# Inversion blocks and inverses read by GpSimd's queue, a chain with fewer slots, and state reads behind the inverses' read

## The chip, the cores and the metric

The kernel runs on one core of a Trainium2 chip. The metric is the device time of one execution in microseconds (us). Names used throughout: PE is TensorE, DVE is VectorE, ACT is ScalarE, POOL is GpSimd, SP is SyncE, which only issues transfers here. SPq, ACTq and POOLq are the queues in which SP, ACT and POOL issue DMAs. POOL is also a compute engine, and it takes its DMAs and its arithmetic from one queue, in order.

## The reference

One inference step of a recurrent decoder trunk with two layers, width 2048, for a prompt of 256 tokens and 8 sample sequences of 8 tokens each, 320 rows in all. What matters here is the first layer, with a gated delta rule of 8 heads (128 x 128) and a gated linear attention (GLA) of 4 heads (128 x 256):

```
proj = rmsnorm(x) @ w_in                  # 2048 -> 7,200 columns
# gated delta rule, per head and per chunk of C tokens
A   = strictly_lower((k * beta) @ k.T * decay)
sol = solve_triangular(A + I, rhs)        # unit diagonal, C x C
v_new = u - w @ S ;  o = (q * exp(G)) @ S + (q @ k.T * decay) @ v_new
S   = S * exp(g_last) + k_dec.T @ v_new
# GLA, per head and per chunk
o = (q * exp(B)) @ S + tril(...) @ v ;  S = diag(exp(b_last)) * S + k_dec.T @ v
x = x + concat(o_a, o_b) * silu(gates) @ w_out
```

The second layer is a gated linear recurrence (RG-LRU) between two more dense products. Every input and result is float32; the outputs are both groups' tokens and all new states.

## The kernel before

**The dense products.** All dense weights (2048 x 512 columns a group, 30 groups of 8 chunks) are streamed from DRAM by SP in chunks of 512 KB (`wst`, line 214). ACT copies each half to float32r (`wh`, line 248), DVE makes the rest (`wl`, line 249), and PE runs three products of 128 x 128 by 128 x 320 for each block: `xh` with `wh`, `xl` with `wh`, `xh` with `wl` (line 381). That is 192 products a group and 5,760 in the loop of line 381. The last group is made by lines 268 to 355.

**The work around them.** All other work is written as Python generators in four lists. After every third dense product `slot()` advances the first generator of each list by one step. Between its steps a generator waits as many slots as the table WAITS has for that place (`yield from wait("invert32.1")`), so that one entry of the table is a delay of three dense products. A scheduler then orders each engine's instructions by that order, by priorities and by what it holds the durations to be; PE executes what it finds in its queue, in order, and stands still if an operand is late. `add_manual_dep(... NoSync ...)` gives the scheduler an order and puts no semaphore into the program.

**The delta rule's inverses.** The prompt's 8 heads are done in two halves of 4 heads, each with two chunks of 128 tokens, c = 0 and 1 (`delta_half`, `quad_prompt`). For a half:

- `quad_a` turns k, q and v, forms k k^T (`kk`, line 786) and k q^T (`kq`, line 798), and writes the four 32 x 32 diagonal blocks of each of its 4 matrices to DRAM (`bd_scratch`, line 793, SP).
- `invert32` reads them back in another layout (`ab`, line 823, four reads), inverts the 32 x 32 blocks by 31 pairs of POOL operations (lines 831 and 833), and writes the inverses to DRAM (`xd_scratch`, line 838, four writes on POOL).
- `load_inv` reads them twice: into `XT` as diagonal blocks (line 871) and into `xc` (line 876).
- `quad_front` builds the 128 x 128 inverse from them: DVE turns `xc` (lines 909 and 919), PE makes `lp` (line 915), DVE copies it to `xp` (line 907), PE makes `lxt` from `xp` and `XT` (lines 925 and 927), and a second, larger step follows (lines 935 and 940). `quad_b` uses the result (`y`, `po`, `sn`, `ks`).

The samples' 8 heads (`delta_sample`) have blocks of 8 x 8, which DVE inverts (line 857 to 861); their inverses go through `xt_scratch` (line 865) into `XT` (line 874). `pq` multiplies the states (`st`, 2 x 512 KB a pair of heads, two buffers, line 1027), and `y` (line 1072) needs `XT` and what DVE makes of `pq`. This is done for two pairs of heads one behind the other.

**GLA's samples.** For each of two pairs of heads: states `st` from DRAM (line 1464), `gpo` (lines 1489 and 1491), then in `gla_out` ACT's square (line 1287), two POOL operations (1288, 1289), DVE's `gon` (1292) and PE's transposes `got` (1296).

**The sum of squares.** Behind the fourth output group, DVE ends the sum `sqa` (line 1594), from which PE makes `r1ps` (line 449) in `row_rstd`.

Of the kernel before, what the change touches and what calls it, by code (L numbers as in the profile page):

```python
# [7 lines left out]
F32 = mybir.dt.float32  # L8
# [6 lines left out]
P = 128  # L15
# [51 lines left out]
def wait(name):  # L67
    for _ in range(WAITS[name]):
        yield
# [3 lines left out]
def hybrid_step(ctx, tc, x_cols, x_rows, w_head, w_dense, w_small, w_lr, w_gate, par_a, par_b, par_c, gains, last_gain,  # L73
# [52 lines left out]
    def behind(i):  # L126
        tc.add_manual_dep(i.ins, marks[-1].name, mybir.DependencyInfo(
            mybir.DependencyClass.NoSync, mybir.DependencyReason.DATA), reason="issue_after")

# [23 lines left out]
    ident = const.tile([P, P], F32, name="ident")  # L153
# [311 lines left out]
    def row_rstd(sq, out, nm):  # L465

        ps = bank4(nm + "ps")
        token_sums(ps, sq, True, True)
        yield from wait("row_rstd.1")
        yield from row_from(ps[:, 0:3, 0], out, nm)  # L470
# [342 lines left out]
    def invert32(ws, first):  # L813
# [8 lines left out]
        for r in range(4):  # L822
            sp.dma_start(ab[32 * r:32 * r + 32].rearrange("p i c -> p (i c)"), bass.AP(
                tensor=bd_d.tensor, offset=bd_d.offset + first * 4 * n * n, ap=[[n * n, 4 * U], [1, n * n]]))
# [42 lines left out]
    def load_inv(q, ws):  # L867
        if q.n == 32:
            for b in range(4):
                bs = slice(32 * b, 32 * b + 32)  # L870
                sp.dma_start(q.xt[bs, :, bs], xd_d[q.id:q.id + 4, b].rearrange("u c i -> c u i"))
        else:
            q.xt = ws.tile([P, 4, P], F32, name="XT", tag="XT")
            sp.dma_start(q.xt, xt_d.rearrange("u p c -> p u c"))
            return
        sp.dma_start(q.xc, xd_d[q.id:q.id + 4].rearrange("u b c i -> (b c) u i"))

# [67 lines left out]
    def quad_b(q, ws, half, c):  # L945
# [13 lines left out]
        ps = bank4("y0")  # L959
        for u in range(U):  # L960
            pe.matmul(ps[:, u, :], q.xt[:, u, :], q.rv[:, u, :], start=True, stop=True)  # L961
# [27 lines left out]
    def delta_half(half):  # L989
        with tc.tile_pool(name=f"gdn{half}", bufs=1, side="right", reuse_waits="tile") as ws:  # L990
# [8 lines left out]
            for c, q in enumerate(qs):  # L999
                q.xt, q.xc = [t_[:, 4 * c:4 * c + 4] for t_ in (xt, xc)]  # L1000
                load_inv(q, ws)
            z = ws.tile([P, 8, 96], F32, name="xz", tag="ab", bufs=1)
            pool.memset(z, 0.0)
            pt = [ws.tile([P, 4, 64], F32, name="xp", tag=tag) for tag in ("xi", "xt")]
            for p_ in pt:
                pool.memset(p_, 0.0)
            yield from wait("quad_b.1")
            yield from quad_front(qs, z[:, :, :64], z[:, :, 64:], pt, xt, xc)
# [5 lines left out]
    def delta_sample():  # L1014
# [3 lines left out]
        with tc.tile_pool(name="gdns", bufs=1, side="right", reuse_waits="tile") as ws:  # L1018
# [4 lines left out]
            def load(u):  # L1023
                st = ws.tile([P, 2, 8, P], F32, name="st", tag="ST", bufs=2)
                sts[u] = st
                for e in range(2):
                    behind(sp.dma_start(st[:, e], state_delta[2 * u + e]))
            load(0)
# [17 lines left out]
            for pr in range(2):  # L1046
# [7 lines left out]
                for v in range(2):  # L1054
                    for a in range(2):
                        for w in range(2):
                            for p in range(4):
                                pe.matmul(pq[32 * p:32 * p + 32, 2 * v + a, :], ms[v][:, a, p, 32 * w:32 * w + 32],
                                          sts[u0 + v][:, a, 2 * p + w, :], start=(v == a == w == 0), stop=False,
                                          tile_position=(0, 32 * p), skip_group_check=True)  # L1060
                for v in range(2):
# [39 lines left out]
                ps = bank4("ot")  # L1101
                for v in range(2):
                    pe.transpose(ps[:, v, :], on[:, v, :], ident)
                for e in range(2):
# [348 lines left out]
    def gla():  # L1453
# [4 lines left out]
        with tc.tile_pool(name="glas", bufs=1, side="right", reuse_waits="tile") as ws:  # L1458
            t = lambda nm, shape, bufs=1: ws.tile(shape, F32, name=nm, tag=nm, bufs=bufs)
            for su in range(2):  # L1460
# [22 lines left out]
                dve.tensor_mul(m, cm, flat(qs16)[:, None, :].to_broadcast([P, 4, P]))  # L1483
                yield from wait("gla.4")
                po = bank("gpo")
# [80 lines left out]
    def evac_res(m):  # L1566
# [16 lines left out]
        def sumsq():  # L1583
# [12 lines left out]
            env["done"].add(("x", m))  # L1596
            if m == 3:
                yield from row_rstd(env["sqa"], rb1, "r1")
                env["done"].add("r1")
                yield from wait("evac_res_sumsq.4")  # L1600
# [499 lines left out]
```

## Time and profile before

| | |
|---|---|
| median of 3 runs | 971.31 us (969.76 to 971.74) |
| profiled execution, device time | 970.0 us |
| its span, first to last instruction | 968.2 us |
| PE busy | 955.2 us, 99% of the span |
| POOL busy | 126.9 us, 13% |
| HBM read, written | 160.02 MB, 14.67 MB |
| granted TensorE clock | 0.998 |

How to read it: the span is what the trace covers, and the device time of the same execution is 1.8 us longer. A row of a group or of the timeline has line, engine, operation, output <- inputs, partitions x elements, count, and what the engine's idle time before it ended with. A row of the chain of waits has the start, the length and what it is. A row of the waits has who waited for whom, then the sum, the number and the longest in us. A row of the windows has the stretch, its length, the busy time of PE, of its weight loads (PEld), DVE, ACT and POOL (with the number of instructions that start in it), the granted clock, the share of the DMA engines and GB/s. Matmuls are pipelined, so a small gap between two of them need not show as idle.

### The profile page before, as it was taken

The numbers are of one execution on the slowest core, as the hardware profiler recorded it, in microseconds if no ns is written. First come the engines' busy times: TensorE is split into PE (matmuls) and PEld (weight loads), VectorE is DVE, ScalarE is ACT, GpSimd is POOL, SyncE is SP. The second block draws the span as 40 slices with busy tenths as digits, with TensorE's granted clock in tenths as the row PEclk, the third lists the DMA queues.
The fourth block names the chain that finished last, engine by engine and source line by source line (L and its number), as shares of the span: only waits on it lengthen the run. The fifth ranks groups of instructions, "written<-read, shape, count | busy, mean of one in ns | idle before, by whom it ended". The sixth has DMA issues, their size and how long they took to land.

```text
span 968.2 us, 18733 instructions
## 1 busy us (share of the span) xinstructions
PE 955.2 (99%) x6942; PEld 939.6 (97%) x6942; DVE 684.0 (71%) x1507; ACT 539.4 (56%) x1094; POOL 126.9 (13%) x294
## 2 busy tenths in 40 slices
PE   9999999999999999999999999999999999999997
PEld 8999999999999998999989999999999999999996
DVE  7599887666545565788667778667969668865763
ACT  6767864547233444876434346348685885434452
POOL 3010108303380011120100000100010000000000
PEclk9999999999999999999999999999999999999999
DMA  9854454523554376444588776645435335578742
GB/s 319 303 174 138 136 150 141 167 92 124 156 159 141 108 231 213 119 138 131 180 307 291 233 246 208 219 155 151 155 119 194 131 114 183 190 273 264 249 156 108
DMA packets 67618, 175.89 MB, mean 182 GB/s; under 512 B 16248, under 2 KB 25208, under 8 KB 67016
## 3 DMA queue, kind: packets, MB, share of 16 engines
q1 hardware_dynamic: 62904, 164.61, 52.7%
q0 software_dynamic: 2560, 8.65, 2.3%
q10 hardware_dynamic: 2064, 1.45, 0.5%
q8 instruction: 54, 0.88, 0.4%
q14 instruction: 36, 0.29, 0.1%
HBM read 160.02 MB, written 14.67 MB: 180 GB/s over the span
## 4 chain that ended last, share of the span: by engine, by line
PE 97%; DMA 2%; DVE 1%; ACT 0%; issue 0%; SPq 0%; POOL 0%; DVEq 0%; ACTq 0%; POOLq 0%
PE acc L381 83%; PE acc L268 3%; DMA wst<-in_w_dense_dram 1%; DMA XT<-xt_scratch 1%; PE fbt L311 1%; PE lg L1678 0%; PE lg L1677 0%; PE lg L1676 0%; PE kq L798 0%; PE kk L786 0%; PE usn L1188 0%; PE po L970 0%; PE y L961 0%; PE gpo L1489 0%; DMA wst<-in_w_head_dram 0%; PE sn L975 0%
## 5 line engine op out<-in xcount | busy, mean ns | idle before, releaser
L381 PE MATMUL acc<-xh,wh 128*128 128x320 f32 x1856 | 580.6, 313 | 0.9 <-ACT wh L235 0.9
L381 PE MATMUL acc<-xl,wh 128*128 128x320 f32 x1856 | 573.9, 310 | 0.0
L381 PE MATMUL acc<-xh,wl 128*128 128x320 f32 x1856 | 572.8, 309 | 0.0
L248 ACT ACTIVATE wh<-wst 128x512 fp32r<-128x512 f32 x479 | 279.2, 624 | 294.8 <-PE acc L381 234.3
L249 DVE TENSOR_TENSOR wl<-wst,wh 128x512 fp32r<-128x512 f32 x479 | 316.9, 691 | 166.2 <-ACT wh L248 165.3
L381 PEld LDWEIGHTS acc<-xh,wh 128*128 128x128 f32 x1856 | 348.6, 188 | 3.7 <-ACT wh L235 1.3
L381 PEld LDWEIGHTS acc<-xl,wh 128*128 128x128 f32 x1856 | 348.5, 188 | 0.7
L381 PEld LDWEIGHTS acc<-xh,wl 128*128 128x128 f32 x1856 | 348.1, 188 | 0.1
L587 DVE SCALAR_TENSOR_TENSOR yc<-slab,pa,yc 128x344 f32<-128x344 f32 x72 | 40.8, 578 | 1.8 <-ACT yc L101 1.5
L831 POOL TENSOR_TENSOR tmp<-ab,xi 128x60 f32<-128x60 f32 (+24 forms) x62 | 23.5, 378 | 55.7 <-DMA wst<-in_w_dense_dram 27.5
L833 POOL TENSOR_TENSOR xi<-xi,tmp 128x60 f32<-128x60 f32 (+24 forms) x62 | 25.5, 412 | 4.9
L1252 POOL DMA_DIRECT2D out_s_gla_dram<-ugt x8 | 4.4, 544 | 113.5 <-DVE ugt L1249 113.5
L1218 POOL DMA_DIRECT2D out_s_delta_dram<-ust x8 | 5.9, 744 | 99.6 <-DVE ust L1215 99.6
L268 PE MATMUL acc<-xl,wh 128*128 128x320 f32 (+1 forms) x64 | 18.7, 292 | 0.0
L268 PE MATMUL acc<-xh,wl 128*128 128x320 f32 (+1 forms) x64 | 18.6, 291 | 0.0
L591 ACT ACTIVATE qkv<-yc 128x256 f32<-128x256 f32 x24 | 9.9, 414 | 15.6 <-DVE yc L587 15.6
L268 PE MATMUL acc<-xh,wh 128*128 128x320 f32 (+1 forms) x64 | 18.6, 291 | 0.0
L1215 DVE SCALAR_TENSOR_TENSOR ust<-ust,es,usn 128x128 f32<-128x128 f32 x64 | 18.1, 340 | 0.1
L1636 DVE SCALAR_TENSOR_TENSOR yc<-slab,pb,yc 128x344 f32<-128x344 f32 x32 | 17.5, 570 | 0.7 <-ACT yc L1634 0.5
L478 DVE TENSOR_TENSOR slab<-acc,rb 128x256 f32<-128x256 f32 x36 | 15.0, 416 | 3.5 <-PE acc L381 3.3
L101 ACT ACTIVATE yc<-slab,pa 128x344 f32<-128x344 f32 x24 | 13.7, 578 | 4.7 <-DVE slab L479 4.5
L1705 POOL MEMSET aa<- 128x32 f32 x4 | 0.7, 171 | 117.7 <-ACT rr L1692 66.7
(464 smaller groups left out, 989.3 us busy)
## 6 DMA issues: line engine op xcount, KB each, us to landing
wst<-in_w_dense_dram SPq DMA_DIRECT2D x237, 512.0 KB, 3.8
st<-in_state_delta_dram SPq DMA_DIRECT2D x8, 512.0 KB, 5.8
st<-in_state_gla_dram SPq DMA_DIRECT2D x4, 1024.0 KB, 4.8
ust<-in_state_delta_dram SPq DMA_DIRECT2D x8, 512.0 KB, 7.5
out_s_delta_dram<-ust POOLq DMA_DIRECT2D x8, 512.0 KB, 6.0
ugt<-in_state_gla_dram SPq DMA_DIRECT2D x8, 512.0 KB
out_s_gla_dram<-ugt POOLq DMA_DIRECT2D x8, 512.0 KB, 4.0
xtok<-in_x_rows_dram SPq DMA_DIRECT2D x6, 512.0 KB, 6.1
```

The lines of the kernel that those rows point to most:

```text
L101: return act.activation(out, in_, AF.Identity, scale=scale)
L248: act.activation(h, wst[i][:, a, :], AF.Copy)
L249: env["last_split"] = dve.tensor_sub(l, wst[i][:, a, :], h.bitcast(F32))
L268: mm = pe.matmul(accs[f][:, cols], w[:, fs], x[:, cols], start=(k == 0 and j == 0), stop=(k == KT - 1 and j == 2), skip_group_check=True)
L381: mm = pe.matmul(o, (h, h, l)[j][:, fs], (xh, xl, xh)[j][k], start=(k == 0 and j == 0), stop=(k == KT - 1 and j == 2))
L478: dve.tensor_mul(xp[:, 3:259], xp[:, 3:259] if acc is None else acc[:, :256], rb[:, :256])
L587: dve.scalar_tensor_tensor(y[:, :n], xp[:, j:j + n], pa[:, ft, j:j + 1], y[:, :n], op0=OP.mult, op1=OP.add)
L591: act.activation(st["t"][:, f, :], y[:, :TP], AF.Silu)
L831: behind(pool.tensor_mul(tv, ab[:, j, j + 1:, None].to_broadcast([P, m, w]), xi[:, j:j + 1, :w].to_broadcast([P, m, w])))
L833: behind(pool.tensor_add(xi[:, j + 1:, :w], xi[:, j + 1:, :w], tv))
L1215: dve.scalar_tensor_tensor(s_, s_, es[:, col:col + 1], ps[b][:, r, :], op0=OP.mult, op1=OP.add)
L1636: dve.scalar_tensor_tensor(y[:, :n], xp[:, j:j + n], pb[:, ft, 2 + j:3 + j], y[:, :n], op0=OP.mult, op1=OP.add)
```

## The change

- **Queues.** The four `ab` reads of a half go from SP's queue to POOL's. The inverses are read on POOL's queue too, and for both chunks of a half at once: one read of `xc` (1,024 runs of 128 bytes) and four of `XT` (256 runs each) in place of two and eight. They are issued behind the memsets of `xz` and `xp`.
- **Slots.** invert32.1 from 18 to 3, invert32.2 from 15 to 13, quad_a.7 from 9 to 6, quad_b.1 from 23 to 20; gla.4 from 16 to 20, with a delay of its own for GLA's second pair (gla.5, 11); evac_res_sumsq.3 is new, 2 slots ahead of `row_rstd`.
- **State reads.** The samples' first four `st` reads have no place in the order given any more; the later four are ordered behind the `XT` read.
- **Order on PE.** The matmuls `y` of a quad in reverse order, `pq` of the second pair behind the first pair's transposes, and those transposes in reverse order.

```
@@ WAITS (changed entries only) @@
-    "quad_a.7": 9, "invert32.1": 18, "invert32.2": 15, "quad_b.1": 23, "gla.4": 16
+    "quad_a.7": 6, "invert32.1": 3, "invert32.2": 13, "quad_b.1": 20, "gla.4": 20, "gla.5": 11,
+    "evac_res_sumsq.3": 2
...
+    def order(i, j):
+        tc.add_manual_dep(i.ins, j.ins.name, mybir.DependencyInfo(
+            mybir.DependencyClass.NoSync, mybir.DependencyReason.DATA), reason="issue_after")
...
         yield from wait("invert32.1")
         for r in range(4):
-            sp.dma_start(ab[32 * r:32 * r + 32].rearrange("p i c -> p (i c)"), bass.AP(
+            pool.dma_start(ab[32 * r:32 * r + 32].rearrange("p i c -> p (i c)"), bass.AP(
                 tensor=bd_d.tensor, offset=bd_d.offset + first * 4 * n * n, ap=[[n * n, 4 * U], [1, n * n]]))
...
     def load_inv(q, ws):
-        if q.n == 32:
-            for b in range(4):
-                bs = slice(32 * b, 32 * b + 32)
-                sp.dma_start(q.xt[bs, :, bs], xd_d[q.id:q.id + 4, b].rearrange("u c i -> c u i"))
-        else:
-            q.xt = ws.tile([P, 4, P], F32, name="XT", tag="XT")
-            sp.dma_start(q.xt, xt_d.rearrange("u p c -> p u c"))
-            return
-        sp.dma_start(q.xc, xd_d[q.id:q.id + 4].rearrange("u b c i -> (b c) u i"))
+        q.xt = ws.tile([P, 4, P], F32, name="XT", tag="XT")
+        q.read = sp.dma_start(q.xt, xt_d.rearrange("u p c -> p u c"))
+
+    def load_blocks(first, xt, xc):
+        us = slice(first, first + 8)
+        pool.dma_start(xc, xd_d[us].rearrange("u b c i -> (b c) u i"))
+        for b in range(4):
+            bs = slice(32 * b, 32 * b + 32)
+            pool.dma_start(xt[bs, :, bs], xd_d[us, b].rearrange("u c i -> c u i"))
...
-        for u in range(U):
+        for u in reversed(range(U)):
             pe.matmul(ps[:, u, :], q.xt[:, u, :], q.rv[:, u, :], start=True, stop=True)
...
             for c, q in enumerate(qs):
-                q.xt, q.xc = [t_[:, 4 * c:4 * c + 4] for t_ in (xt, xc)]
-                load_inv(q, ws)
+                q.xt = xt[:, 4 * c:4 * c + 4]
...
             for p_ in pt:
                 pool.memset(p_, 0.0)
+            load_blocks(8 * half, xt, xc)
             yield from wait("quad_b.1")
...
                 for e in range(2):
-                    behind(sp.dma_start(st[:, e], state_delta[2 * u + e]))
+                    i = sp.dma_start(st[:, e], state_delta[2 * u + e])
+                    if u > 1:
+                        order(i, q.read)
+                        behind(i)
...
-                                pe.matmul(pq[32 * p:32 * p + 32, 2 * v + a, :], ms[v][:, a, p, 32 * w:32 * w + 32],
-                                          sts[u0 + v][:, a, 2 * p + w, :], start=(v == a == w == 0), stop=False,
-                                          tile_position=(0, 32 * p), skip_group_check=True)
+                                i = pe.matmul(pq[32 * p:32 * p + 32, 2 * v + a, :], ms[v][:, a, p, 32 * w:32 * w + 32],
+                                              sts[u0 + v][:, a, 2 * p + w, :], start=(v == a == w == 0), stop=False,
+                                              tile_position=(0, 32 * p), skip_group_check=True)
+                                if pr:
+                                    order(i, q.turned)
...
-                for v in range(2):
-                    pe.transpose(ps[:, v, :], on[:, v, :], ident)
+                for v in (1, 0):
+                    q.turned = pe.transpose(ps[:, v, :], on[:, v, :], ident)
...
-                yield from wait("gla.4")
+                yield from wait("gla.5" if su else "gla.4")
...
             if m == 3:
+                yield from wait("evac_res_sumsq.3")
                 yield from row_rstd(env["sqa"], rb1, "r1")
```

How the instructions move. SP's queue around the reads of the first half's inverses, before the change:

```order
L214 DMA wst<-in_w_dense_dram 128x1024 x6
L871 DMA XT<-xd_scratch 32x4x32 x4
L876 DMA xc<-xd_scratch 128x4x32
L871 DMA XT<-xd_scratch 32x4x32 x4
L876 DMA xc<-xd_scratch 128x4x32
L214 DMA wst<-in_w_dense_dram 128x1024 x2
```

POOL's queue at the same place in the change (`xp` and `xz` are the front's operands, `slab` belongs to a dense group):

```order
L1006 MEMSET xz 128x768
L839 COPY xt<-xi 128x256
L842 DMA xd_scratch<-xt 256x1x32 x4
L1009 MEMSET xp 128x256 x2
L877 DMA xc<-xd_scratch 128x8x32
L880 DMA XT<-xd_scratch 32x8x32 x4
L509 MEMSET slab 128x4x3
L510 COPY slab<-pa 128x4x8x3
```

The ten reads leave SP's queue, and five stand on POOL's, behind the writes that they read from and ahead of the slab's memset. SP's queue around the samples' inverses, before:

```order
L850 DMA ab<-bt_scratch 16x8x8 x4
L214 DMA wst<-in_w_dense_dram 128x1024 x2
L865 DMA xt_scratch<-ab 16x8x8 x4
L214 DMA wst<-in_w_dense_dram 128x1024
L1027 DMA st<-in_state_delta_dram 128x1024
L874 DMA XT<-xt_scratch 128x4x128
L1027 DMA st<-in_state_delta_dram 128x1024 x3
```

and in the change:

```order
L854 DMA ab<-bt_scratch 16x8x8 x4
L218 DMA wst<-in_w_dense_dram 128x1024
L1125 DMA kt_scratch<-ktm 4x32x128 x2
L218 DMA wst<-in_w_dense_dram 128x1024 x2
L869 DMA xt_scratch<-ab 16x8x8 x4
L873 DMA XT<-xt_scratch 128x4x128
L1031 DMA st<-in_state_delta_dram 128x1024 x4
```

The read of `XT` now follows the `xt_scratch` writes at once, and all four state reads come behind it. On PE the same matmuls are issued, at other places between the dense products. The number of dense products of line 381 (385 in the change) that PE has ahead of the first matmul named:

| matmul | before | in the change |
|---|---|---|
| half 0: second `kq`, `lp`, `lxt` | 734, 1171, 1191 | 734, 1092, 1099 |
| half 1: second `kq`, `lp`, `lxt` | 1391, 1827, 1837 | 1316, 1674, 1681 |
| samples, first pair: `pq`, `y` | 2109, 2133 | 1947, 1993 |
| samples, second pair: `pq`, `y` | 2184, 2208 | 2022, 2046 |
| GLA's samples, first pair: `gpo`, `got` | 2752, 2762 | 2615, 2637 |
| GLA's samples, second pair: `gpo`, `got` | 2799, 2809 | 2670, 2688 |
| `r1ps` | 3552 | 3558 |

8 rows, old and new, of the table WAITS are left out of this document.

## The prediction

> **What bounds the kernel now.** I read the page's busy row and its chain first, then PE's waits, then PE's idle time window by window.
>
> ```profile
> PE 955.2 (99%) x6942; PEld 939.6 (97%) x6942; DVE 684.0 (71%) x1507; ACT 539.4 (56%) x1094; POOL 126.9 (13%) x294
> PE 97%; DMA 2%; DVE 1%; ACT 0%; issue 0%; SPq 0%; POOL 0%; DVEq 0%; ACTq 0%; POOLq 0%
> ```
>
> The chain is TensorE from end to end. No matmul is added or removed, so only the 13.0 us in which PE is idle (968.2 - 955.2) can be won, and any new wait on PE costs its full length. The next two views say who ends that idle time and where it lies.
>
> ```profile
> PE y L1072 <- DMA XT<-xt_scratch: 2.4, 1, 2.4
> PE frs L353 <- DVE rr L351: 1.4, 1, 1.4
> PE got L1296 <- DVE gon L1292: 1.2, 2, 0.6
> PE warm L1831 <- DVE mhalf L1815: 1.1, 1, 1.1
> PE acc L381 <- ACT wh L235: 0.9, 1, 0.9
> PE r1ps L449 <- DVE sqa L1594: 0.5, 1, 0.5
> ```
>
> ```profile
> 0.00:10.00 10.00, 8.04 (x44) 7.64 (x45) 5.69 (x13) 6.03 (x11) 5.26 (x14) 1.00 0.80 234
> 360.00:380.00 20.00, 17.62 (x170) 16.89 (x169) 12.26 (x36) 9.43 (x22) 2.65 (x7) 1.00 0.69 226
> 490.00:510.00 20.00, 18.77 (x157) 16.81 (x156) 15.49 (x39) 6.28 (x13) 1.28 (x3) 1.00 0.95 353
> 610.00:620.00 10.00, 9.50 (x67) 9.23 (x66) 5.26 (x8) 3.15 (x6) 0.89 (x1) 1.00 0.84 306
> 950.00:968.20 18.20, 11.26 (x74) 9.62 (x72) 9.13 (x20) 5.27 (x13) 0.73 (x1) 0.90 0.38 144
> ```
>
> The start (1.96 us idle) and the end (6.94) are not touched. Three middle windows hold 20 - 17.62 = 2.38, 20 - 18.77 = 1.23 and 10 - 9.50 = 0.50 us: the waits for XT, got and r1ps. That is 4.11 us, and the change reaches all three.
>
> **The sample inverses, XT (2.38).** The chain of waits around 363 us, the timeline's rows ahead of it, and two rows of DMA landings:
>
> ```profile
> 361.35 0.20 DVE L861 COPY ab<-xi 64x64 f32<-64x64 f32 x1
> 361.58 1.75 SPq L865 DMA_DIRECT2D xt_scratch<-ab  x4
> 363.33 1.05 PE pq L1058 x32
> 364.40 0.35 SPq L1027
> 364.93 6.25 DMA XT<-xt_scratch
> 371.31 0.68 PE y L1072 x4
> 380.56 1.89 PE pq L1058 x64
> xt_scratch<-ab SPq DMA_DIRECT2D x4, 4.0 KB, 1.5
> DMA to landing us min/median/max: 4.4/4.8/7.1
> ```
>
> On SP a 512 KB state read stands ahead of the XT read and is held until pq has freed its buffer (364.38), so XT goes out at 364.93 and its 256 KB share the DMA engines with that read. In the change the XT read stands right behind the xt_scratch writes and all four state reads behind it. The last write is issued near 362.9 and lands 1.5 us later, so XT can go out near 364.5 instead of 364.93; with the same 6.25 us it lands 9.4 us behind the copy's start at 361.35. In PE's order y now stands 46 dense products behind pq instead of 24. A product costs 0.1467 us (64.09 / 437, quoted below), so even if pq again starts 1.98 us behind that copy, y falls due at 1.98 + 1.05 + 46 x 0.1467 = 9.8 us, and later if pq does. The wait ends without any help from a faster read: -2.38. What is late next are the state reads, which the second pq needs. The last goes out about 6 us behind the copy and lands at most 7.1 later, at 13; the second pq stands 75 products behind the first (11.0 us) with 2.6 us of other matmuls between, at 15.6. Covered by 2.6 us.
>
> **The GLA output, got (1.23), and r1ps (0.50).**
>
> ```profile
> 488.46 0.63 PE gpo L1491 x2
> 491.17 0.44 PE got L1296 x2
> 125.36 64.09 PE acc L381 x437
> ```
>
> From the end of gpo (489.09) to got are 2.08 us: ScalarE's square, two GpSimd operations, VectorE's gon. PE has ten products there, 1.47 us, so it waits 0.61; the second pair is alike. In the change 22 and 18 products stand between, 3.23 and 2.64 us, both over 2.08: -1.23. r1ps moves six products back, 0.88 us against a wait of 0.50: -0.50. Neither moves a DMA.
>
> **The block inversions' reads on POOL (cost 0 to 6.6, taken as 0).** This is where the change can lose. Per half it takes four ab reads and ten reads of the inverses off SP and puts four and five on POOL, and it shortens the way from the second kq to lp from 437 products (half 0) and 436 (half 1) to 358, 52.5 us. Timeline rows of POOL and SP in both halves, PE's chain rows, and the landings of POOL's xd_scratch writes:
>
> ```profile
> 130.21 0.31 SPq L823 DMA_DIRECT2D ab<-bd_scratch  x1
> 144.93 0.39 POOL L831 TENSOR_TENSOR tmp<-ab,xi 128x31 f32<-128x31 f32 x1 [27.50 <-DMA wst<-in_w_dense_dram]
> 176.90 2.60 POOL L838 DMA_DIRECT2D xd_scratch<-xt  x4 [0.31 <-POOL xt L835]
> 182.36 0.31 POOL L1006 MEMSET xp<- 128x256 f32 x1 [2.54 <-DMA xd_scratch<-xt]
> 242.01 63.94 PE acc L381 x436
> 256.52 0.61 POOL L831 TENSOR_TENSOR tmp<-ab,xi 128x31 f32<-128x31 f32 x1 [23.55 <-DMA ab<-bd_scratch]
> 286.87 2.42 POOL L838 DMA_DIRECT2D xd_scratch<-xt  x4 [0.30 <-POOL xt L835]
> 290.69 0.31 POOL L1006 MEMSET xp<- 128x256 f32 x1 [1.08 <-DMA xd_scratch<-xt]
> L838 POOL DMA_DIRECT2D xd_scratch<-xt x8: 596/630/847, 176.9 to 288.6; - x8
> DMA to landing us min/median/max: 1.9/3.0/4.1
> ```
>
> Half 0: the blocks are in DRAM at 130.21, when SP's first read got through. Four issues on POOL at 0.65 and a landing of 2.4 behind the last issue's end (3.0 - 0.6) start the inversion at 135.2 instead of 144.93. From its first operation to the first xd_scratch write are 176.90 - 144.93 = 31.97 us: 167.2. To the landing another 5.46: 172.6, and 0.3 for the memset: 172.9. The xc read moves 1024 runs where an xd_scratch write moves 256. No row has that; bounds are 0.65 (runs are free) and 2.6 (four times), and I take 1.4, nearer to the one-write row. xc lands at 176.7, and two transposes (0.89, below) make lp ready at 177.7. It is due at 125.36 + 52.5 = 177.9. The four XT reads add 2.6: landed at 179.3, against lxt's due time of 177.9 + 0.6 + 7 x 0.1467 = 179.5. Both fit by 0.2 us.
>
> Half 1: the blocks again 4.85 us behind kq's end (130.21 - 125.36; the change leaves no weight load between those writes), inversion start at 9.8, then 286.87 - 256.52 = 30.35 and 3.82 + 0.3: 44.3; XT landed at 50.7 against 54.1. Slack 3.4.
>
> The bounds: with the fastest landing (1.9) everything is early, worth nothing since PE waits for none of it now. With 0.85 per issue, 3.4 for xc and 4.1 for landings, ab is 1.6 late and the last XT read 3.5 more: 5.1 - 0.2 = 4.9 stall in half 0, 5.1 - 3.4 = 1.7 in half 1, 6.6 together. I take 0, the median rows. The relief of SP earns nothing: PE waits for no weight load. Queued behind the waiting reads on POOL are the slab's memset and copy, which come earlier than now, as the whole chain does.
>
> **A tighter front (+0.8).** The front's lp and lxt stand closer.
>
> ```profile
> 303.32 0.89 DVE L909 STREAM_TRANSPOSE xz<-xc 32x256 f32<-32x256 f32 x2
> 305.95 0.63 PE lp L915 x32
> 306.58 1.66 PE acc L381 x10
> 306.95 1.00 DVE L907 COPY xp<-lp 32x128 f32<-32x128 f32 x4
> ```
>
> From lp's end to lxt are 1.66 us, filled by ten products (1.47 unhindered, so 0.19 is lost already). Seven give 1.03: 0.63 short, or 0.26 if the copies start 0.37 sooner. Two halves less the 0.19: 0.3 to 1.1, taken as 0.8, since VectorE has weight differences ahead of the copies again.
>
> **Sum.** -2.38 - 1.23 - 0.50 + 0.8 = -3.3. The span goes from 968.2 to 964.9, the profiled execution from 970.0 to 966.7. The median of the runs shown is 1.3 above that execution, so the forecast is 968.0.
>
> **Rivals.**
>
> *The inverses come late.* For it: the 0.2 us of slack in half 0, on a landing whose row spreads from 1.9 to 4.1. Against it: half 1's slack, and reads that no longer share a queue with weight loads. Half of the bound, 2.5 us, gives 970.5: within 0.2% of the median, which is about what a measurement of this kernel can tell from no change.
>
> *The change doesn't do what it says at XT.* If XT still waits, because the read itself stays at 6.25 us or longer and pq starts early, or the state reads stop the second pq instead, 2 us come back: 970.0. Against it stand the 22 added products (3.2 us).
>
> *Slower: POOL issues are held up by VectorE.*
>
> ```profile
> L831 POOL TENSOR_TENSOR tmp<-ab,xi x62: 205/298/825, 144.9 to 284.4; 128x60 f32<-128x60 f32 x6, 128x28 f32<-128x28 f32 x4, 128x54 f32<-128x54 f32 x4, 128x48 f32<-128x48 f32 x4
> ```
>
> One and the same operation takes 205 to 825 ns, so POOL is held up at times. If its reads take twice the 0.65 us (and xc 2.8), each half is 2.6 + 1.4 + 2.6 = 6.6 us later: 6.4 stall in half 0, 3.2 in half 1, 977.6. It decides once a half is about 4.5 us late, a read at 1.1 us: then 4.3 + 1.1 eat the gain of 3.3 and 0.2% more. Against it: the eight xd_scratch writes, issued while VectorE split weights, never took over 847 ns. [...]
>
> **How the numbers follow.** Forecast 0.62 (966 to 969.3), late inverses 0.18, XT still late 0.08, slower 0.12. With the better edge of the second, faster by over 0.2% gets 0.66, within 0.2% gets 0.21, slower 0.13. The range: without the tighter front's 0.8 and with a median 1.3 nearer to the profiled execution 965.9; upwards to 973.0, the forecast and 5 of the 6.6 us of late landings, which leaves out the slower rival.
>
> **What would show it.** Right: in the changed profile no wait of y on XT, of got on gon, of r1ps on sqa; XT issued ahead of every st read; POOL's reads at 0.6 to 0.9 us with xc near 1.4; lp and lxt near 1.4 us apart; PE idle of 9 to 10 us. Wrong: a wait of lp on the transposes or of lxt on XT; xc over 2.6 us on POOL; the second pq waiting on st; or inversions that start later than 10 us behind kq.

## The result: slower by 1.25%

The kernel before takes 970.53 us at the median and the changed one 982.56: ratio 1.0125, 95% interval 1.0107 to 1.0142. The forecast of 968.0, its range up to 973.0 and the sign were wrong. The profiled execution went from 970.0 us (span 968.2) to 983.5 (span 981.7). Of these 13.5 us PE stands still for 7.0 (13.0 became 981.7 - 961.7 = 20.0), and is busy for 6.5 longer with the same instructions. The busy row of the changed kernel's page, and its view of PE's waits:

```profile
PE 961.7 (98%) x6942; PEld 944.5 (96%) x6942; DVE 682.3 (69%) x1507; ACT 536.8 (55%) x1092; POOL 149.7 (15%) x312
```

```profile
PE lp L919 <- DVE xz L913: 7.1, 4, 3.8
PE ot L1112 <- DVE on L1107: 1.4, 2, 1.2
PE frs L357 <- DVE rr L355: 1.4, 1, 1.4
PE warm L1841 <- DVE mhalf L1825: 1.1, 1, 1.1
PE y L1081 <- DMA XT<-xt_scratch: 0.9, 1, 0.9
PE lxt L929 <- issue: 0.6, 1, 0.6
```

The rows of `got` and `r1ps` are gone, XT's fell from 2.4 to 0.9, a row of `ot` is new, and above all stands `lp`, which before did not wait. The windows around the fronts of both halves (the column ahead of the last two is the granted clock):

```profile
180.00:190.00 10.00, 6.79 (x95) 6.16 (x96) 5.89 (x13) 1.95 (x4) 2.06 (x6) 0.58 0.45 134
190.00:200.00 10.00, 10.00 (x84) 9.32 (x84) 3.46 (x7) 3.40 (x11) 0.00 (x0) 0.91 0.21 57
285.00:295.00 10.00, 7.06 (x49) 6.79 (x47) 1.29 (x2) 2.31 (x4) 6.66 (x12) 0.96 0.45 134
295.00:305.00 10.00, 9.00 (x130) 7.95 (x131) 6.07 (x14) 2.01 (x4) 0.04 (x1) 0.70 0.40 114
```

Behind each standstill the clock is lower (0.58 and 0.70 over ten microseconds). PE was busy for 13.6 us at half clock, from 181.57 to 191.81 and from 294.21 to 301.03; half of that, 6.8 us as an estimate, is about the 6.5 by which it was busy longer. The timeline's rows of the chain, half 0 and then half 1:

```profile
124.74 1.06 PE L802 MATMUL kq<-qkv 128*128 128x128 f32 x8
131.21 2.28 POOL L827 DMA_DIRECT2D ab<-bd_scratch  x4 [13.35 <-PE acc L385]
139.17 0.24 POOL L835 TENSOR_TENSOR tmp<-ab,xi 128x31 f32<-128x31 f32 x1 [5.68 <-DMA ab<-bd_scratch]
172.36 1.29 DVE L253 TENSOR_TENSOR wl<-wst,wh 128x512 fp32r<-128x512 f32 x2 [1.00 <-ACT wh L252]
172.42 2.33 POOL L842 DMA_DIRECT2D xd_scratch<-xt  x4 [0.29 <-POOL xt L839]
178.50 0.93 POOL L877 DMA_DIRECT2D xc<-xd_scratch  x1 [0.17 <-issue]
181.93 0.90 DVE L913 STREAM_TRANSPOSE xz<-xc 32x256 f32<-32x256 f32 x2 [8.28 <-DMA xc<-xd_scratch]
182.88 1.06 PE L919 MATMUL lp<-xz,bt 128*32 128x32 f32 x30 [0.15 <-DVE xz L913]
183.32 2.50 DVE L253 TENSOR_TENSOR wl<-wst,wh 128x512 fp32r<-128x512 f32 x4
238.50 1.06 PE L802 MATMUL kq<-qkv 128*128 128x128 f32 x8
242.54 0.68 DVE L792 TENSOR_TENSOR bt<-kk,dtm 128x512 f32<-128x512 f32 x1
248.36 2.09 POOL L827 DMA_DIRECT2D ab<-bd_scratch  x4 [18.33 <-DMA bd_scratch<-bt]
256.39 0.24 POOL L835 TENSOR_TENSOR tmp<-ab,xi 128x31 f32<-128x31 f32 x1 [5.94 <-DMA ab<-bd_scratch]
285.79 2.34 POOL L842 DMA_DIRECT2D xd_scratch<-xt  x4 [0.30 <-POOL xt L839]
296.31 1.06 PE L919 MATMUL lp<-xz,bt 128*32 128x32 f32 x30 [0.15 <-DVE xz L913]
```

POOL issues its reads quickly (0.57 us each, `xc` 0.93), but the inversion starts only 8.0 us behind the first issue. And VectorE reached the transposes at 173.65, stood 8.28 us until `xc` had landed, and only then (from 183.32) made the four weight differences that stand behind them.

### The profile page after: what moved, and what is told of

The parts are those of the page before. It is cut to its first block, busy times and chain, and to the rows that moved or that the text cites. A ratio compares the mean times of both kernels' runs of the same rounds, so it can differ in the third digit from the quotient of the medians.

```text
span 981.7 us, 18741 instructions
## 1 busy us (share of the span) xinstructions
PE 961.7 (98%) x6942; PEld 944.5 (96%) x6942; DVE 682.3 (69%) x1507; ACT 536.8 (55%) x1092; POOL 149.7 (15%) x312
## 4 chain that ended last, share of the span: by engine, by line
PE 84%; POOL 7%; DMA 4%; issue 2%; DVE 1%; ACT 1%; SPq 0%; DVEq 0%; POOLq 0%; ACTq 0%
PE acc L385 71%; POOL xi L837 3%; POOL tmp L835 3%; PE acc L272 3%; DMA ab<-bd_scratch 1%; DMA xd_scratch<-xt 1%; PE fbt L315 1%; PE lg L1688 0%; PE lg L1687 0%; PE lg L1686 0%; DMA wst<-in_w_head_dram 0%; PE usn L1197 0%; PE y L965 0%; DMA xt_scratch<-ab 0%; PE gpo L1498 0%
```

## The experiments

Every diff is against the changed kernel, unless it says the kernel before. Nothing is left out of any computation; where matmuls are added, `lp` overwrites their results. Ratios are to the kernel before on the same chip, with their 95% interval.

### lp later; the clock; the old slots; the old queue

My first theory was that the slots were cut below the chain's length, and that the halved clock is the other half of the loss; the rival, that reads on POOL's queue cost by themselves.

```
lp_later:        -"quad_b.1": 20                +"quad_b.1": 30
fill10:          ahead of the first lp, in each half:
                 +for _ in range(10):
                 +    pe.matmul(ps[:, 0:2, :], ident, ident, start=True, stop=True)
old_slots:       quad_a.7 9, invert32.1 18, invert32.2 15, quad_b.1 23 (as before)
short_slots_sp:  the kernel before with quad_a.7 6, invert32.1 3, invert32.2 13, quad_b.1 20
```

> The change with one entry different: quad_b.1 from 20 to 30, so that 388 dense products instead of 358 stand between the second kq and lp in both halves, 30 x 0.1467 = 4.4 us more. Queues and all else as in the change. Theory (the change cut the wait budget of lp below the length of the chain through DRAM, and PE's standstill halves its clock afterwards): the 7.1 us of waits of lp on the transposes are gone or under 0.5, the granted clock is 1.00 in the windows of both fronts, PE busy is back near 955, and the time is 982.6 - 7.1 - 6.5 = 969, give or take 1 for the waits of y and ot in the samples, which shift. Rival (the reads on POOL's queue cost time by themselves, wherever lp stands): no better than 978.

Measured: 979.4 us, 1.0077 (1.0059 to 1.0096). The number is the rival's, but its cause is neither theory's. `lp` no longer waits, something else does. PE's waits, and timeline rows of the first front (of the profiled execution, with 984.3 us the longest of four; the shortest took 977.4):

```profile
PE acc L385 <- DVE smpvb L1282: 3.4, 1, 3.4
PE acc L385 <- DVE wl L253: 2.9, 1, 2.9
```

```profile
183.56 0.88 DVE L913 STREAM_TRANSPOSE xz<-xc 32x256 f32<-32x256 f32 x2 [8.57 <-DMA xc<-xd_scratch]
184.93 2.50 DVE L253 TENSOR_TENSOR wl<-wst,wh 128x512 fp32r<-128x512 f32 x4
185.67 0.64 PE L385 MATMUL acc<-xh,wl 128*128 128x320 f32 x1 [2.88 <-DVE wl L253]
```

The entry moved `lp` on PE, but the transposes kept their place in VectorE's order. VectorE waits for the landing as long as ever (8.57 us), and now it is the dense products that run out of `wl` (and, in the second front, of accumulators that VectorE has not emptied, `smpvb`). The standstill has changed its name.

> The change with ten more matmuls (128 x 128 by 128 x 128, float32, from data that is long there, into the bank that lp overwrites) ahead of lp in each half: about 3.1 us of PE work that falls into the standstill of 3.5 and 4.2 us and makes nothing earlier. Theory: lp starts when it did, so the standstill costs the same 7 us, but PE is busy in it, the clock stays at 1.00, the dense products behind lp take 0.147 us instead of 0.267, and the 6.5 us by which PE's other work was slower are won: 976 (975 to 977.5). Rival (the clock falls for a reason of its own, a place in the program or the power that is drawn): the clock is 0.50 behind lp again and the time stays at 982 to 983, or is longer by what the ten matmuls cost.

Measured: 981.4 us, 1.0104 (1.0089 to 1.0119): 2 us less than the change, of which the intervals leave little certain, and not 6.5. The ten matmuls took 2.39 us, not 3.1. The clock stayed at 1.00 in the first half, and there PE now waited 2.0 us ahead of `lxt`:

```profile
182.86 2.50 DVE L253 TENSOR_TENSOR wl<-wst,wh 128x512 fp32r<-128x512 f32 x4
185.39 1.00 DVE L911 COPY xp<-lp 32x128 f32<-32x128 f32 x4
186.29 0.22 PE L931 MATMUL lxt<-XT,xp 128*32 128x32 f32 x2 [1.95 <-issue]
```

The copies that `lxt` needs are queued behind the four late `wl`. What the clock gave here, VectorE took (1.95 us ahead of `lxt`).

> The change with the four entries of the delta rule's chain as before (quad_a.7 9, invert32.1 18, invert32.2 15, quad_b.1 23); reads on POOL's queue, state reads, GLA's and row_rstd's entries as in the change. 436 dense products stand between the second kq and lp again, and in the samples y and ot stand where they stood before (24 and 72 products behind pq). Theory: no wait of lp, clock 1.00 throughout, got and r1ps still without a wait (1.7 us won), and XT between all and nothing won: 967 to 970.5. Rival (POOL's reads cost by themselves): over 975.

Measured: 968.9 us, 0.9982 (0.9971 to 0.9993), with a granted clock of 0.999. So POOL's queue cost nothing here, where the old slots leave room for it. `got` still waited for 1.2 us, against the expectation: with the longer chain the GLA's tail has ten products between `gpo` and `got` as before. It is the shorter chain that pays for that gain.

> The kernel before with only the four entries of the delta rule's chain as in the change (quad_a.7 6, invert32.1 3, invert32.2 13, quad_b.1 20): the same 358 products between kq and lp, but all reads on SP's queue, behind the weights' reads. Theory (the budget is what costs; POOL's queue made the chain shorter, not longer): lp is later than in the change, by up to the 5.8 us by which the inversion started later before, the standstill is 4 to 10 us in each half, the clock falls to 0.50 behind each, and the time is 983 to 1000. Rival (the reads on POOL's queue are what costs): 968 to 973.

Measured: 977.0 us, 1.0061 (1.0046 to 1.0076), between the two. The sign of my theory holds (short slots cost without POOL's reads, too), but its aside on the queue was the wrong way round. By SP's queue the inversion starts 4.8 us sooner, and `lp` waits less than in the change. The inversion's first operation, and the wait:

```profile
134.35 0.59 POOL L831 TENSOR_TENSOR tmp<-ab,xi 128x31 f32<-128x31 f32 x1 [16.96 <-DMA ab<-bd_scratch]
```

```profile
PE lp L915 <- DVE xz L909: 4.7, 4, 2.7
```

### VectorE's place of the transposes, and the blocks by SP's queue

The theory became: the inverses are late for two readers, VectorE's queue and PE's `lp`, and both have to be mended; and POOL's queue makes them late.

```
turn_pin:      -    dve.transpose(dst[cut(b)], xc[cut(b)])
               +    behind(dve.transpose(dst[cut(b)], xc[cut(b)]))
               -dve.transpose(x[cut(1), :, n:], xc[cut(1)])
               +behind(dve.transpose(x[cut(1), :, n:], xc[cut(1)]))
lp_later_pin:  turn_pin, and quad_b.1 30
ab_sp:         -pool.dma_start(ab[32 * r:32 * r + 32]...
               +sp.dma_start(ab[32 * r:32 * r + 32]...
ab_sp_pin:     turn_pin and ab_sp
```

> The change with VectorE's three transposes of xc put behind the current slot in the order given, so that four more weight differences (wl) stand ahead of them and none is stuck behind; lp stays 358 products behind kq. Theory, as the last four runs have changed it: two things are late by one landing, VectorE's queue (the transposes reach their place 8 us before xc has landed, and the wl behind them wait too) and PE's lp. With only the first mended lp still stands still for about 3.5 us in each half, since xc lands when it did, and the clock still halves: 980 to 982.5, about the change. Rival (VectorE's blocked queue is all): 970 or better.

Measured: 979.5 us, 1.0095 (1.0072 to 1.0117), a little better than expected; `lp` waits for 8.3 us in sum. The edit did less than I expected of it. In the trace no four weight differences come ahead of the transposes: two stand between them in half 0 and one in half 1, and VectorE still waits for 6.3 and 5.9 us at the first of them (8.3 and 8.05 in the change).

> The same order on VectorE and lp 388 products behind kq (quad_b.1 30): both mended. With lp alone later (the run before) the time was 979.4, because PE then waited for wl behind the blocked transposes. Theory: no standstill over 1 us at either front, no wait of acc on wl there, clock 1.00 in all windows of the middle, PE busy about 955: 969 (968 to 970.5). Rival (reads on POOL's queue cost by themselves, or PE's order is what costs): 977 or more, as with lp later alone.

Measured: 972.2 us, 1.0011 (0.9999 to 1.0023). By the ratios lp later alone won 4.7 us on the change, VectorE's order alone 2.9, the two together 11.1, which is 3.5 more than the sum; the four intervals together leave about as much open. The windows of the two fronts and VectorE's row of the first:

```profile
175.00:190.00 15.00, 15.00 (x181) 14.27 (x179) 8.72 (x20) 4.85 (x10) 4.83 (x10) 1.00 0.65 196
285.00:310.00 25.00, 25.00 (x262) 23.69 (x260) 14.11 (x35) 9.93 (x24) 4.59 (x7) 1.00 0.40 117
182.27 0.90 DVE L913 STREAM_TRANSPOSE xz<-xc 32x256 f32<-32x256 f32 x2
```

PE is busy without a gap, at full clock, and the transposes wait for nothing. What is left above the forecast of 969 lies in the samples and GLA, where all later work shifted (`ot` 2.1, `acc` on `wh` 1.2, `y` on `wl` 1.1, `got` 1.1).

> The change with only the four ab reads of a half back on SP's queue; slots, and the reads of the inverses on POOL, as in the change. Where these reads went by SP with the same slots, the inversion started at 134.35 and 249.91 instead of 139.17 and 256.39. Theory (the chain is late because the reads by POOL's queue land late, 5.6 us behind their last issue instead of 2.5): the chain ends 4.8 and 6 us sooner, lp is ready before it is due, VectorE waits some 3 us instead of 8 at its transposes, the clock stays up: 969 (968 to 971.5). Rival (the reads of the inverses on POOL, or the slots alone, keep it late): a wait of lp of over 2 us is left in a half, and 974 or more.

Measured: 975.3 us, 1.0046 (1.003 to 1.0062). By 7.7 us better than the change, but not the 969: the inversion started at 134.64, 4.5 us sooner, and its first write came at 169.77, only 2.7 sooner (35.13 us of inverting against 33.25). `lp` still waited for 2.8 us and `lxt` for 2.5, and the clock of 180 to 190 was 0.66.

> The two together: the ab reads back on SP's queue and VectorE's transposes behind the current slot; slots as in the change. Theory: as with the reads alone, and nothing stuck behind the transposes on VectorE, so lxt comes without the copies' delay too: 967.5 (966.5 to 969.5), faster than the kernel before by got's 1.2 us, r1ps's 0.5 and what XT and ot leave of 2.4. Rival (the gains of got, r1ps and XT are eaten elsewhere): 970 to 972, no change to the kernel before.

Measured: 973.4 us, 1.0029 (1.0017 to 1.0041); `lp` waited for 3.6. Both expectations missed: with the chain at 358 products SP's queue is not enough either.

### All together; the clock again; the samples' reads alone

```
combined:    ab_sp_pin, and quad_b.1 25, quad_out.1 7, gla.4 12, gla_out.4 8,
             y of a quad in its old order, and in the samples
             -yield from wait("delta_sample.4")
             +yield from wait("delta_sample.4" if pr else "delta_sample.9")    # 8, and 15
fill10_pin:  turn_pin and fill10
xt_only:     the kernel before with
             -behind(sp.dma_start(st[:, e], state_delta[2 * u + e]))
             +i = sp.dma_start(st[:, e], state_delta[2 * u + e])
             +if u > 1:
             +    order(i, q.read)
             +    behind(i)
```

> The change's slots where they earn something and room where they cost: ab on SP's queue, VectorE's transposes behind the current slot, lp 373 products behind kq instead of 358 (quad_b.1 25, 2.2 us more; with the reads and the order alone lp still waited for up to 1.9 us a half), y of a quad in its old order, seven more slots between pq and y of the samples' first pair so that ot is 36 products behind pq's second part again and not 23, quad_out.1 10 to 7 and gla.4 20 to 12 to pay for it, gla_out.4 4 to 8. Theory (all that the change lost was these late operands): no wait of lp, ot, got over 0.3 us, clock 1.00 in the middle, PE idle of about 10 us on 955 busy, a span of 965.5, 968 (967 to 969.5). Rival (something else in the change costs): 971 or more.

Measured: 967.0 us, 0.9961 (0.9949 to 0.9973), faster than both kernels. Its longest waits of PE:

```profile
PE frs L357 <- DVE rr L355: 1.4, 1, 1.4
PE warm L1841 <- DVE mhalf L1825: 1.1, 1, 1.1
PE acc L385 <- ACT wh L239: 1.0, 1, 1.0
PE y L1081 <- DMA XT<-xt_scratch: 0.9, 1, 0.9
PE lxt L929 <- DMA XT<-xd_scratch: 0.5, 2, 0.3
```

No `lp`, `ot`, `got`, `r1ps`. With these operands in time nothing of the loss is left. Several entries and orders were changed at once here, so this shows their sum and not the share of each.

> The change with VectorE's transposes behind the current slot (979.5 when that alone was changed) and ten more matmuls ahead of lp in each half. There PE was busy 958.7 us, 3.7 more than the 955.0 of a run at full clock. Theory (standing still halves the clock, and with VectorE's queue free nothing hides the gain): the clock stays at 1.00 in both fronts and 3 to 4 us are won, 976 (975 to 977); lp starts when it did. Rival (the clock is not it, or what comes behind lp is bound by VectorE's copies anyway): 979 to 980.

Measured: 979.1 us, 1.0088 (1.0073 to 1.0103), no difference to 979.5. This time the clock stayed at 1.00 in the second half and fell in the first (0.50 from 184 to 186 us).

> The kernel before with only the samples' reads in the change's order: the read of XT straight behind the xt_scratch writes, and the four later state reads behind it. Every entry of the table, and pq and y (24 products apart), as before. Theory (the state read that went ahead of XT shared the DMA engines with it, 6.25 us instead of 2.9 in the change): XT lands 3 us sooner, y no longer waits or for less than 0.5, the state reads are still in time for the second pq: 2.0 to 2.4 us won, ratio 0.9977. Rival (the read starts no earlier, as its issue waits for the writes to land, and stays at 6 us): no difference, ratio 0.9995 to 1.0005.

Measured: 967.7 us, 0.9971 (0.996 to 0.9982), as the theory had it, and not told apart from the combined version. SP's queue and PE:

```profile
363.51 1.75 SPq L869 DMA_DIRECT2D xt_scratch<-ab  x4
366.41 0.38 SPq L878 DMA_DIRECT2D XT<-xt_scratch  x1
366.89 1.87 SPq L1031 DMA_DIRECT2D st<-in_state_delta_dram  x4
370.70 0.61 PE L1079 MATMUL y<-rv,XT 128*128 128x128 f32 x4
```

At most 4.3 us lie between the read's issue and `y`, which does not wait. By itself this part of the change won 2.8 us, where the combined version won 3.8.

### What the clock costs, and why the blocks land late

```
fill15_pin:  turn_pin, with 15 matmuls ahead of lp in each half
ab_act:      -pool.dma_start(ab[32 * r:32 * r + 32]...
             +act.dma_start(ab[32 * r:32 * r + 32]...
```

> As the last run with more matmuls ahead of lp and VectorE's transposes behind the current slot, but with 15 in place of ten: 15 x 0.24 = 3.6 us of PE work in a standstill of 3.9 and 5.0 us. There ten (2.4 us) left 1.6 us of standing still ahead of lp, and the clock fell in the first half and not in the second. Theory (what is left to stand still is too short to be taken for idleness): the clock stays at 1.00 in both fronts, the 3.7 us are won that PE was busy longer than at full clock when only the transposes had been moved, and 979.5 becomes 976 (975 to 977.5). Rival (the matmuls make lp late themselves, or what follows is bound by other engines): 978.5 or more.

Measured: 979.3 us, 1.0087 (1.0061 to 1.0113). PE was busy 963.1 us, 7.0 of them the added matmuls, so 956.1 in place of 958.7, but without the added matmuls the rest of the span was 2.2 us longer (977.2 - 956.1 against 977.6 - 958.7). Again the clock held in one half (1.00 in the first) and fell in the other (0.56 from 294 to 296 us), where 1.6 us of standing still were left ahead of `lp`.

> The change with the four ab reads of a half on ACT's queue. Not the time counts here (ACT's weight copies wait behind reads that wait for the blocks), but from a read's issue to its landing and the start of the inversion. If it is POOL's queue that is slow: landing at 2.7 to 3.3 us at the median, as on SP's queue, though the weights' reads run beside them. If it is the weights' reads that run beside them: 4.5 to 6.5, as on POOL's.

One execution, 980.6 us. The blocks' reads (KB each, median us from issue to landing) of the change, of the kernel before with short slots, and of this kernel:

```profile
ab<-bd_scratch POOLq DMA_DIRECT2D x8, 128.0 KB, 5.2
```

```profile
ab<-bd_scratch SPq DMA_DIRECT2D x8, 128.0 KB, 2.7
```

```profile
ab<-bd_scratch ACTq DMA_DIRECT2D x8, 128.0 KB, 5.0
```

By ACT's queue they land as late as by POOL's. In three other profiles with the short slots it was 4.9 us (`lp_later`) and 6.6 (`turn_pin`) by POOL's queue and 3.1 by SP's (`ab_sp`). So it is not something that only POOL's queue has. What the two slow ones share is the traffic. SP issues its first weight read of 512 KB at 132.66 in the change and at 132.19 here, among the reads of the blocks (131.21 to 133.49, and 131.40 to 133.19). With the blocks on SP's queue (the run above with nothing else changed) it goes out at 132.57, behind the last of them (130.49 to 132.20). No run holds the weights back alone, so this cause is read from the order of the issues and not tested.

## Why the prediction was wrong

**The block inversions, taken as 0, cost nearly everything.** Four steps of that term failed.

- *"a landing of 2.4 behind the last issue's end"*, taken from POOL's small `xd_scratch` writes. The inversion started 5.7 us behind it in half 0 (131.21 + 2.28 to 139.17) and 5.9 in half 1. By the order of the issues, and not tested, the longer time belonged to reads beside weight traffic (5.2 us, against 3.1 by SP's queue with nothing else changed). The kernel before had a row of these very reads, four times as large as the writes and with a median of 4.2 us from issue to landing instead of 3.0:

```profile
ab<-bd_scratch SPq DMA_DIRECT2D x8, 128.0 KB, 4.2
```

  In half 0 `lp` was ready 57.1 us behind kq's end instead of 52.3. Of these 4.8 us, 3.3 are the landing and 1.3 the inversion, which took 33.25 us instead of 31.97.
- *"Half 1: the blocks again 4.85 us behind kq's end"*. POOL got its first read through at 5.4 us in half 0 (125.80 to 131.21), but at 8.8 in half 1 (239.56 to 248.36). There VectorE made `bt` only at 242.54, 3.0 us behind kq's end and behind what it had for a dense group; before the change it was 0.9 (242.94 and 242.01). The inversions started 13.4 and 16.8 us behind kq, where I had 9.8, and "later than 10" had been named as a sign of failure.
- *"It is due at 125.36 + 52.5"*: the due time was read on PE. The landing's first reader is VectorE, which works ahead of PE and reached the transposes 5.7 us before PE reached `lp` (173.65 and 179.4). The four weight differences behind them on VectorE waited too (until 183.32), which the prediction had asked for POOL's queue and not for VectorE's. This is why moving `lp` alone only moved the wait. Moving the transposes alone left VectorE waiting for 6 us, and with both moved no wait of either was left.
- The bound of 6.6 us was too low. `lp` alone waited for 7.1, since the bound's largest landing (4.1) came from the same wrong rows, and what VectorE's wait and the clock cost beside it was not in the bound.

**The second cost is the clock, for which the prediction had no term, and its price stays open.** In each of the three fills the clock stayed at 1.00 in one half, where in the change it fell to 0.50 in both. The fills do not show that this wins time: 2.0, 0.7 and 0.8 us by the ratios to their partners, none beyond the intervals, where 6.5, 3 to 4 and 3.7 were expected. Nor do they settle the price, since in each profile the clock fell in the other half, and VectorE still waited at the transposes, for 6.3 to 8.8 us in the first and the third. In the first fill the copies behind VectorE's late `wl` took what the clock gave. Two of the four executions with 15 matmuls had a granted clock of 0.999 over the whole span, and took 979.64 and 979.65 us, no less than the 979.42 to 979.59 of three executions without the matmuls at 0.993. So no run here shows that the 6.5 us by which PE was busy longer could have been won alone.

**The samples' XT, -2.38: mechanism right, sum wrong.** By itself the order of the reads won 2.8 us (the run with it alone). In the change XT's wait only fell to 0.9, as rows of its timeline and of its DMA issues show:

```profile
354.85 1.96 PE L1065 MATMUL pq<-st,qm 128*32 128x128 f32 x64
355.88 0.20 DVE L865 COPY ab<-xi 64x64 f32<-64x64 f32 x1
361.67 0.39 SPq L873 DMA_DIRECT2D XT<-xt_scratch  x1
```

```profile
xt_scratch<-ab SPq DMA_DIRECT2D x4, 4.0 KB, 3.3
```

The step *"even if pq again starts 1.98 us behind that copy"* did not hold: `pq` came 1.0 us ahead of the copy, three microseconds the other way, and the writes took 3.3 us to land instead of 1.5. The read itself was as quick as hoped: 2.9 us from its issue to the end of `y`'s wait, where it had been 6.25. The sum also took 1.05 us for `pq`, which is the row of 32 of its 64 matmuls; all take 1.95, so `y` would have been due 0.9 later than it says. And one wait was overlooked. The change moved `y` 22 products back but `ot` only two, so that 23 products (3.4 us) in place of 36 stood ahead of `ot` for a chain of 4.6 us (366.98 to 371.59): a new wait of 1.2. The sum of the two is about nothing.

**got (-1.23) and r1ps (-0.50) were right**: no row of either is left. **The tighter front (+0.8)** has its row, 0.6 ahead of `lxt` in half 0.

**The rivals.** "The inverses come late" had the place, but 2.5 us of the 14.6 by which the forecast was missed. "Slower" had the sign and, with 977.6, came nearest, but not its mechanism: POOL's reads took 0.5 to 0.8 us, `xc` 0.93, never twice the price. Its row of 205 to 825 ns mixes 25 shapes (one shape alone, 128x31, took 390 and 610 ns in the kernel before).

## What to carry to other kernels

When an operand comes by a transfer, look up its first reader and read the due time in that engine's own queue; an engine that prepares work for PE can run microseconds ahead (5.7 here), and one early place in its order can hold up what stands behind it (four weight differences behind a wait of 8.28 us here). Price a transfer by its own row, or by one of its size with the same traffic beside it: when the blocks' reads left the weights' queue, a weight read went out among them (132.66, between 131.21 and 133.49) and not behind the last, and they landed at 5.2 us instead of 3.1. And move a consumer on every engine that it has a part on, since moving it on one only gave the wait another name here (7.1 us at `lp` became 3.4 and 2.9 at `acc`).

## What was not expected of the hardware

- Behind standstills of 3.5 and 4.2 us (from the last dense product's end to `lp`'s second row, 182.88 and 296.31) the granted clock was 0.50. In half 0 it stayed there until 191.81, and dense products started 0.27 us apart instead of 0.147:

```profile
184.00:186.00 2.00, 2.00 (x7) 1.71 (x7) 1.97 (x5) 0.00 (x0) 0.00 (x0) 0.50 0.30 33
188.00:190.00 2.00, 2.00 (x8) 2.00 (x9) 1.10 (x2) 1.82 (x4) 0.00 (x0) 0.50 0.48 188
```

  The two stretches at half clock lasted 10.24 and 6.82 us, and their starts lie 112.64 us apart: three, two and 33 times 3.41 us. In the profiles of the fills the clock was low behind one front for 3.4 us, once in each. In the last 3.41 us ahead of both returns in the change PE had no gap (188.40 to 191.81 and 297.62 to 301.03). Ahead of the five falls of the table it had not been without work: in the last 3.41 us it was busy for 1.24 to 1.86. The stretches of the table are 3.41 us long and lie whole multiples of that from the changes of the clock in the same trace; this choice is the author's, and no run shows that the clock goes by such stretches:

| run | stretch, us | PE busy in it, us | clock behind it |
|---|---|---|---|
| the change | 178.16 to 181.57 | 1.24 | 0.50 |
| the change | 290.80 to 294.21 | 1.26 | 0.50 |
| ten matmuls, transposes moved | 180.31 to 183.72 | 1.25 | 0.50 |
| 15 matmuls, transposes moved | 290.85 to 294.26 | 1.60 | 0.50 |
| blocks by SP's queue | 178.05 to 181.46 | 1.86 | 0.50 |
| the kernel before | 367.14 to 370.55 | 1.79 | 1.00 |
| ten matmuls | 182.50 to 185.91 | 1.84 | 1.00 |
| ten matmuls, transposes moved | 289.53 to 292.95 | 1.91 | 1.00 |

  So the length of a wait alone does not decide: a wait of 1.6 us ahead of `lp` kept the clock at 1.00 with ten matmuls and ended at 0.50 with 15 (both in half 1, with the transposes moved), and the 2.4 us ahead of `y` before the change kept it. Nor does the table show a border: with 1.86 us of work the clock fell, with 1.79 and 1.84 it stayed. What decides is not shown.

- An inversion of the same 62 operations took 32.0 to 35.1 us in the first half of the prompt's heads and 29.4 to 30.4 in the second (the kernel before, the change, `short_slots_sp`, `ab_sp` and `ab_sp_pin`). In the first it took 35.1 in the last three, which have the short slots and the blocks by SP's queue and start it earliest (134.35 to 136.08), and 33.3 in the change, where the blocks came by POOL's queue (139.17). What made the difference was not tried.
